# Five transposes per feature block of x, the keys' bank copied by ScalarE, and a later split of the cached values

## The chip, the cores and the metric

The kernel runs on one core of a Trainium2 chip, in one launch. The metric is device time in microseconds (us), as the median of repeated executions. Shown beside it is one execution taken with the hardware profiler, whose rows are quoted below.

## What is computed

The reference is one inference step of a streaming encoder with one layer. Its parts, cut to what matters here:

```python
h = rmsnorm(x, norm_attn_g)                       # x: 16 meta + 512 prompt rows, and 64 sample rows, 2048 features
z = h @ w_in                                      # columns: qd | kd | vd (8 heads x 128 each) | cq | ckv | krope
# group A: differential attention, 8 heads, two 64-wide halves each
s = einsum(qd, kd) * DIFF_SCALE + t5_bias         # chunk-causal mask; the sample also reads 128 cached keys
p = softmax(s)[half 0] - lam * softmax(s)[half 1]
o_d = rmsnorm(p @ vd) * (1 - lam_init)
# group B: latent attention with a rotary key; then
x = x + concat(o_d, o_m) @ w_out
x = x + (silu(h2 @ w_gate) * (h2 @ w_up)) @ w_down
y = rmsnorm(x)
# outputs: y, and the new rows of kd, vd, ckv and krope in their natural layout (tokens x columns)
```

All arithmetic is in fp32. The kernel forms each fp32 product from three faster ones of split operands (high times high, high times low, low times high).

## The kernel before

All 592 tokens (512 prompt, 64 sample, 16 meta) are kept as columns: a feature block is a tile of 128 features x 592 tokens. The change touches the first quarter of the program.

**The x stage** (`load_x`, `transpose_x`, `project_both`). Rows of x are loaded in groups of 512 features into tiles `xn`. For each of the 16 feature blocks, `transpose_x` lets TensorE transpose the pieces of x into one PSUM tile `pxt` of two banks, with half of the tokens (296) at the start of each bank. That is why there are six pieces: 128, 128, 40 tokens in the first bank, 108, 108 and 80 in the second. ScalarE then writes the scaled high part `xh`, VectorE the low part `xl` and a plain copy `xt`, which goes to memory (`xspill`). Two `pxt` tiles exist, so a block's transposes wait until VectorE has copied the `xt` of two blocks ago. ScalarE also squares the pieces (`junk`) for the row sums of the norm; `ss`, reduced by VectorE after the last group, becomes the factor `rc` per token. Between the transposes TensorE projects the first head's queries and keys (`ps`).

**The row factors** (`first_rows`). TensorE turns `rc` into rows (`prb`), one product for each piece, VectorE copies them to `rb`, and every projection is multiplied by it.

**A head of group A.** `projections` emits, for each head, the products of queries, keys and values in eight-block halves. Beside it run tasks: `twin_queries` and `stack_keys` split operands into high and low parts (`q00h`, `q00l`, `kk`); `keys` and `values` call `natural`, which transposes the new rows back to tokens x columns, copies the full bank of the 512 prompt tokens to `na` and stores it (`pna`, `na`), then does the same with the 80 other tokens (`pnb`, `nb`); `diff_attend` makes scores (`sp`, two banks), exponentials (`e`), probabilities (`p`) and products with the values (`po`). The transposes of `natural`, the cached keys' (`pck`), the probabilities' and the gains' (`pg`) share one PSUM bank, called "tp".

**What sets the order.** TensorE's order is the program's: a planner, `Streams`, keeps a model clock and picks the next task by rank and by the time its buffers are due, and TensorE's instructions are kept in that order. The other engines' instructions are placed by the compiler's scheduler, which uses its own costs. Each engine then works through its list in order, and waits at the head of it. Loads and stores go out on SP's queue, which is also in order; GpSimd issues the broadcasts of the bias table (`tsk<-trow`, one for each head), from which `bias` is loaded.

Of the kernel before, what the change touches and what calls it, by code (L numbers as in the profile page):

```python
# [116 lines left out]
def encoder_step(  # L117
# [181 lines left out]
    def ev(ps, n=TH):  # L299
        return ps[:, :, 0:n]  # L300
# [18 lines left out]
    with ExitStack() as ph:  # L319
# [33 lines left out]
        tok = [(0, P), (P, P), (256, 40), (TH, 108), (404, 108), (SEQ, OWN)]  # L353
        ps0, ps1 = pjt(), pjt()
        with tc.tile_pool(name="xn", bufs=1, reuse_waits="tile") as xn:
            first_gain = xn.tile([KC, P], F32, name="first_gain")
            S.dma_start(first_gain, g_attn.rearrange("(c p) -> c p", p=P))
            ssp = az.tile([P, 6, 4], F32, name="ssp")
# [4 lines left out]
            def load_x(cg):  # L363
                cs = slice(cg * 512, (cg + 1) * 512)
                for j in (0, 1, 2, 3, 5):
                    o, n = tok[j]
                    t = xn.tile([P, 1 + (j == 3), 512], F32, name="xn", tag=f"xn{j}", bufs=3)
                    second_queue = S.dma_start if cg == 0 and j in (1, 2, 5) else load
                    if j == 5:
                        second_queue(t[0:NS, 0], x_sample[:, cs])  # L370
                        second_queue(t[NS:OWN, 0], meta[:, cs])
                    elif j == 3:
                        load(t[0:n], x_prompt[o:o + 2 * n, cs].rearrange("(a p) c -> p a c", p=n))
                        xt_in[cg, 4] = t[:, 1]
                    else:
                        second_queue(t[0:n, 0], x_prompt[o:o + n, cs])
                    xt_in[cg, j] = t[:, 0]

            def transpose_x(kc):
                cg, k = kc // 4, kc % 4  # L380
                sp = sbig("pxt")
                for j, (o, n) in enumerate(tok):
                    b = o // TH
                    PE.transpose(sp[:, b, o - b * TH:o - b * TH + n],
                                 xt_in[cg, j][0:n, k * P:(k + 1) * P], ident[0:n, 0:n])
                xt = ztile("xt")
                split_scaled(hv(xh[kc]), hv(xl[kc]), ev(sp), gA[:, kc:kc + 1])
                V.tensor_copy(hv(xt), ev(sp))
                for o, n, c in KEPT:
                    store(xspill[kc, :, c:c + n], xt[:, o:o + n])  # L390
                for j in ((0, 1), (2, 3), (4,), (5,))[k]:
# [55 lines left out]
            ss = az.tile([P, 6], F32, name="ss")  # L447
            rc = az.tile([P, 6], F32, name="rc")
# [31 lines left out]
        def natural(src32, dst_p, dst_s, keep):  # L480
# [6 lines left out]
            V.tensor_copy(na, pa.rearrange("p (j c) -> p j c", j=4))  # L487
# [13 lines left out]
        def keys(h, z, kk):  # L501
# [4 lines left out]
            yield from natural(z, nk_p[:, c], nk_s[:, c], lambda na, nb: None)  # L506
# [22 lines left out]
        def values(h, z, vh, vl):  # L529
# [3 lines left out]
            split(vh[:, 5, :], vl[:, 5, :], cv)  # L533
# [1159 lines left out]
```

## Time and profile before

| | |
|---|---|
| median of 3 runs | 2409.49 us (2408.25 to 2411.52) |
| the profiled execution | 2406.11 us, its span 2404.3 us |
| busy in the span: TensorE, VectorE, ScalarE, GpSimd | 98%, 78%, 47%, 31% |
| x stage with the first head's projections | from 0 us to the first `prb` at 67.44 us |
| the eight heads of group A | from there to about 530 us |
| latent attention, output projection, feed-forward | from about 530 us to the end |

A row in order of time gives start, duration, engine, line, operation and tiles, and in brackets how long the engine stood idle before and what ended that. A row of a group gives count, busy time, mean in ns, and idle time ahead of it. Matmuls overlap, so the time that one holds TensorE's list is read from the start of the next, not from its duration.

### The profile page before, as it was taken

What the parts mean: (1) busy time and instruction counts of PE and PEld (TensorE: products, weight loads), DVE (VectorE), ACT (ScalarE), POOL (GpSimd) and SP (SyncE); (2) the same over time, 40 slices, a digit from 0 to 9 for tenths busy, and PEclk for the clock granted to TensorE, in tenths of its full rate; (3) what the DMA queues carried; (4) which work ended last, traced back from release to release, by engine and by line L of the source; (5) the groups of instructions that cost most, each with busy time, mean ns of one, the idle gap of its engine ahead of it and who ended that gap; (6) DMA issues with size and microseconds to landing.
All of it is one profiled execution on the core that took longest, in us unless ns stands there. A gap on an engine that the chain in (4) does not pass through costs nothing. (4 is left out here: it accounts for less than half of the span.)

```text
span 2404.3 us, 43647 instructions
## 1 busy us (share of the span) xinstructions
PE 2344.6 (98%) x17336; PEld 2305.3 (96%) x17336; DVE 1886.0 (78%) x2750; ACT 1127.8 (47%) x1999; POOL 740.7 (31%) x463
## 2 busy tenths in 40 slices
PE   7999999999999999999999999999999999999998
PEld 6999999989998999999999999999999999999997
DVE  5666677676665788888888888888888788888884
ACT  5455554444444554444445545445444333333435
POOL 0100000130000356465455455555554222222220
PEclk9999999999999999999999999999999999999999
DMA  7533333253333543444454454445345984744522
GB/s 217 146 91 96 85 89 96 75 155 118 112 103 108 179 150 116 155 158 130 151 165 135 140 165 147 138 155 162 127 151 174 323 285 145 242 164 152 193 89 97
DMA packets 360372, 353.10 MB, mean 147 GB/s; under 512 B 23906, under 2 KB 316392, under 8 KB 360168
## 3 DMA queue, kind: packets, MB, share of 16 engines
q1 hardware_dynamic: 358374, 345.47, 45.5%
q0 software_dynamic: 1296, 4.07, 0.5%
q8 instruction: 136, 2.23, 0.4%
q10 hardware_dynamic: 498, 0.78, 0.1%
q14 instruction: 68, 0.56, 0.1%
HBM read 268.82 MB, written 82.34 MB: 146 GB/s over the span
## 5 line engine op out<-in xcount | busy, mean ns | idle before, releaser
L1234 PE MATMUL m<-b,wh 128*128 128x288 f32 x7280 | 1061.6, 294 | 6.2 <-ACT wh L157 2.9
L1234 PEld LDWEIGHTS m<-b,wh 128*128 128x128 f32 x7280 | 995.4, 188 | 9.0 <-ACT wh L157 4.9
L1238 PE MATMUL m<-b,wl 128*128 128x288 f32 x3640 | 583.2, 296 | 4.3 <-DVE wl L154 3.0
L154 DVE TENSOR_TENSOR wl<-raw,wh 128x1024 fp32r<-128x1024 f32 (+2 forms) x347 | 509.5, 1469 | 40.7 <-ACT wh L157 40.3
L1238 PEld LDWEIGHTS m<-b,wl 128*128 128x128 f32 x3640 | 514.3, 188 | 10.2 <-DVE wl L154 9.1
L157 ACT ACTIVATE wh<-raw 128x1024 fp32r<-128x1024 f32 (+2 forms) x347 | 313.6, 904 | 367.2 <-PE m L1234 320.1
L1220 POOL TENSOR_TENSOR ws<-raw 128x512 f32<-128x512 f32 (+2 forms) x124 | 224.9, 1814 | 615.3 <-DVE wl L154 361.2
L157 ACT ACTIVATE wh<-ws 128x512 fp32r<-128x512 f32 (+2 forms) x248 | 196.6, 793 | 284.9 <-PE m L1234 113.6
L154 DVE TENSOR_TENSOR wl<-ws,wh 128x512 fp32r<-128x512 f32 (+2 forms) x248 | 250.1, 1008 | 7.7 <-PE m L1238 4.4
L109 PE MATMUL ps<-xh,wh 128*128 128x296 f32 (+1 forms) x992 | 223.8, 307 | 1.6 <-DVE ls L586 1.2
L109 PE MATMUL ps<-xl,wh 128*128 128x296 f32 (+1 forms) x992 | 215.8, 299 | 0.5 <-DVE xl L162 0.5
L109 PE MATMUL ps<-xh,wl 128*128 128x296 f32 (+1 forms) x960 | 208.0, 298 | 0.0
L1384 DVE TENSOR_TENSOR c<-c,s 128x288 fp32r<-128x288 f32 x172 | 170.8, 993 | 0.0
L1492 DVE TENSOR_TENSOR y<-y,m 128x288 f32<-128x288 f32 x280 | 125.7, 449 | 50.5 <-PE m L1238 50.5
L109 PEld LDWEIGHTS ps<-xh,wh 128*128 128x128 f32 x992 | 160.7, 190 | 4.3 <-ACT wh L157 1.4
L109 PEld LDWEIGHTS ps<-xl,wh 128*128 128x128 f32 x992 | 161.5, 189 | 0.9 <-DVE xl L162 0.9
L109 PEld LDWEIGHTS ps<-xh,wl 128*128 128x128 f32 x960 | 156.0, 189 | 0.0
L1220 POOL TENSOR_TENSOR raw<-raw 128x1024 f32<-128x1024 f32 (+1 forms) x46 | 143.2, 3114 | 3.5
L157 ACT ACTIVATE wh<-wr 128x1024 fp32r<-128x1024 f32 (+1 forms) x110 | 101.6, 924 | 87.2 <-PE ps L109 58.6
L154 DVE TENSOR_TENSOR wl<-wr,wh 128x1024 fp32r<-128x1024 f32 (+1 forms) x108 | 116.0, 1074 | 28.9 <-ACT wh L157 26.8
L1330 DVE TENSOR_TENSOR c<-c,m 128x288 f32<-128x288 f32 x171 | 73.1, 447 | 77.9 <-PE m L1238 47.7
L1403 POOL TENSOR_TENSOR c<-c,rb 128x576 f32<-128x576 f32 x44 | 74.9, 1703 | 138.1 <-ACT c L1402 138.1
(364 smaller groups left out, 3030.1 us busy)
## 6 DMA issues: line engine op xcount, KB each, us to landing
raw<-in_ffn_w_gate SPq DMA_DIRECT2D x44, 1024.0 KB, 9.3
raw<-in_ffn_w_up SPq DMA_DIRECT2D x44, 1024.0 KB, 7.3
b<-opspill SPq DMA_DIRECT2D x147, 288.0 KB, 6.0
raw<-in_ffn_w_down SPq DMA_DIRECT2D x32, 1024.0 KB, 5.7
wr<-in_w_in SPq DMA_DIRECT2D x57, 512.0 KB, 4.0
opspill<-s SPq DMA_DIRECT2D x43, 576.0 KB, 3.1
opspill<-c SPq DMA_DIRECT2D x43, 576.0 KB, 5.7
raw<-in_ffn_w_down SPq DMA_DIRECT2D x8, 1280.0 KB, 6.2
```

The source lines that it names most:

```text
L109: self.tc.keep_in_program_order(self.pe.matmul(out, lhsT, rhs, start=start, stop=stop))
L154: V.tensor_tensor(lo, src, f32(hi), op=ALU.subtract)
L157: S.activation(hi, src, AF.Copy)
L1220: (G if p in (5, 7) else V).tensor_tensor(x, y, z, op=ALU.add if p == 5 else ALU.subtract)
L1234: PE.matmul(banks[p], wh[:, k, :], x, start=first and new and k == 0 and x is hi, stop=False, skip_group_check=not new)
L1238: PE.matmul(banks[p], wl[:, k, :], hi, start=False, stop=last and k == n - 1, skip_group_check=not new)
L1330: V.tensor_tensor(c, c, banks[p], op=ALU.add)
L1384: V.tensor_tensor(src[:, k].bitcast(F32R), src[:, k], f32(hi[:, k]), op=ALU.subtract))
L1403: G.tensor_tensor(g[:, f, :], g[:, f, :], rb2, op=ALU.mult)
L1492: V.tensor_tensor(c, c, banks[p], op=ALU.add)
```

## The change

Three edits.

1. x is cut into five pieces of 128, 128, 128, 128 and 80 tokens, placed one after the other in `pxt` (512 columns in the first bank, 80 in the second). So a feature block has five transposes in place of six, a group of 512 features is loaded with two large and two small transfers (in the first group four of 128 rows, two of them from ScalarE's queue), there are 20 squares in place of 24, and `first_rows` makes five products in place of six and copies 512 and 80 columns in place of 296 and 296.
2. `natural` is handed its copy: for keys the full bank `pna` is copied to `na` by ScalarE, for values by VectorE as before.
3. In `values`, the split of the cached values `cv` is written at the end of the task, not after its load.

```diff
@@ -350,45 +350,42 @@
         V.memset(ones, 1.0)
 
 
-        tok = [(0, P), (P, P), (256, 40), (TH, 108), (404, 108), (SEQ, OWN)]
+        tok = [(0, P), (P, P), (2 * P, P), (3 * P, P), (SEQ, OWN)]
         ps0, ps1 = pjt(), pjt()
         with tc.tile_pool(name="xn", bufs=1, reuse_waits="tile") as xn:
             first_gain = xn.tile([KC, P], F32, name="first_gain")
             S.dma_start(first_gain, g_attn.rearrange("(c p) -> c p", p=P))
-            ssp = az.tile([P, 6, 4], F32, name="ssp")
+            ssp = az.tile([P, 5, 4], F32, name="ssp")
             V.memset(ssp, 1.0)
             junk = xn.tile([P, 512], F32, name="junk")
             xt_in = {}
 
             def load_x(cg):
                 cs = slice(cg * 512, (cg + 1) * 512)
-                for j in (0, 1, 2, 3, 5):
-                    o, n = tok[j]
-                    t = xn.tile([P, 1 + (j == 3), 512], F32, name="xn", tag=f"xn{j}", bufs=3)
-                    second_queue = S.dma_start if cg == 0 and j in (1, 2, 5) else load
-                    if j == 5:
-                        second_queue(t[0:NS, 0], x_sample[:, cs])
-                        second_queue(t[NS:OWN, 0], meta[:, cs])
-                    elif j == 3:
-                        load(t[0:n], x_prompt[o:o + 2 * n, cs].rearrange("(a p) c -> p a c", p=n))
-                        xt_in[cg, 4] = t[:, 1]
+                for j in (0, 2):
+                    t = xn.tile([P, 2, 512], F32, name="xn", tag=f"xn{j}", bufs=3)
+                    if cg:
+                        load(t, x_prompt[j * P:(j + 2) * P, cs].rearrange("(a p) c -> p a c", p=P))
                     else:
-                        second_queue(t[0:n, 0], x_prompt[o:o + n, cs])
-                    xt_in[cg, j] = t[:, 0]
+                        for i, queue in enumerate((load, S.dma_start)):
+                            queue(t[:, i], x_prompt[(j + i) * P:(j + i + 1) * P, cs])
+                    xt_in[cg, j], xt_in[cg, j + 1] = t[:, 0], t[:, 1]
+                t = xt_in[cg, 4] = xn.tile([OWN, 512], F32, name="xn", tag="xn4", bufs=3)
+                second_queue = load if cg else S.dma_start
+                second_queue(t[0:NS], x_sample[:, cs])
+                second_queue(t[NS:OWN], meta[:, cs])
 
             def transpose_x(kc):
                 cg, k = kc // 4, kc % 4
-                sp = sbig("pxt")
+                sp = sbig("pxt").rearrange("p a b -> p (a b)")[:, 0:T]
                 for j, (o, n) in enumerate(tok):
-                    b = o // TH
-                    PE.transpose(sp[:, b, o - b * TH:o - b * TH + n],
-                                 xt_in[cg, j][0:n, k * P:(k + 1) * P], ident[0:n, 0:n])
+                    PE.transpose(sp[:, o:o + n], xt_in[cg, j][0:n, k * P:(k + 1) * P], ident[0:n, 0:n])
                 xt = ztile("xt")
-                split_scaled(hv(xh[kc]), hv(xl[kc]), ev(sp), gA[:, kc:kc + 1])
-                V.tensor_copy(hv(xt), ev(sp))
+                split_scaled(xh[kc], xl[kc], sp, gA[:, kc:kc + 1])
+                V.tensor_copy(xt, sp)
                 for o, n, c in KEPT:
                     store(xspill[kc, :, c:c + n], xt[:, o:o + n])
-                for j in ((0, 1), (2, 3), (4,), (5,))[k]:
+                for j in ((0,), (1,), (2,), (3, 4))[k]:
                     n = tok[j][1]
                     S.activation(junk[0:n], xt_in[cg, j][0:n], AF.Square, accum_out=ssp[0:n, j, cg:cg + 1])
                 if kc == 3:
@@ -444,8 +441,8 @@
                 project_both(kc)
                 if kc + 2 < KC:
                     transpose_x(kc + 2)
-            ss = az.tile([P, 6], F32, name="ss")
-            rc = az.tile([P, 6], F32, name="rc")
+            ss = az.tile([P, 5], F32, name="ss")
+            rc = az.tile([P, 5], F32, name="rc")
             V.reduce_sum(ss, ssp, axis=AX.X)
             V.tensor_scalar(ss, ss, 1.0 / D, EPS, op0=ALU.mult, op1=ALU.add)
             rsqrt(rc, ss)
@@ -477,14 +474,14 @@
         p5 = ap.tile([P, 2 * P], F32, name="p5")
         G.memset(p5, 0.0)
 
-        def natural(src32, dst_p, dst_s, keep):
+        def natural(src32, dst_p, dst_s, keep, copy):
 
             yield from st.take("tp")
             pa = tbank("pna")
             for j in range(4):
                 PE.transpose(pa[:, j * P:(j + 1) * P], src32[:, j * P:(j + 1) * P], ident)
             na = ap.tile([P, 4, P], F32, name="na", tag="na")
-            V.tensor_copy(na, pa.rearrange("p (j c) -> p j c", j=4))
+            copy(na, pa.rearrange("p (j c) -> p j c", j=4))
             store(dst_p[NM:NM + SEQ, :].rearrange("(j p) c -> p j c", p=P), na)
             st.give("tp", 1.9)
             yield 1.0
@@ -503,7 +500,8 @@
             ck = ap.tile([P, P], F32, name="ck", tag="ck", bufs=2)
             load(ck, cache_k[:, c])
             yield 2.0
-            yield from natural(z, nk_p[:, c], nk_s[:, c], lambda na, nb: None)
+            yield from natural(z, nk_p[:, c], nk_s[:, c], lambda na, nb: None,
+                               lambda out, bank: S.activation(out, bank, AF.Copy))
             yield from st.take("tp")
             pk = tbank("pck")
             PE.transpose(pk[:, 0:P], ck, ident)
@@ -530,7 +528,6 @@
             c = slice(h * P, (h + 1) * P)
             cv = ap.tile([P, P], F32, name="cv", tag="ck", bufs=2)
             load(cv, cache_v[:, c])
-            split(vh[:, 5, :], vl[:, 5, :], cv)
             yield 1.2
 
             def keep(na, nb):
@@ -538,7 +535,8 @@
                 stack_own(vh[:, 0, :], nb[0:NS])
                 meta_values(vmt[h % 2], nb[NS:OWN])
 
-            yield from natural(z, nv_p[:, c], nv_s[:, c], keep)
+            yield from natural(z, nv_p[:, c], nv_s[:, c], keep, V.tensor_copy)
+            split(vh[:, 5, :], vl[:, 5, :], cv)
             yield 1.5
 
         rows = 23
@@ -690,11 +688,11 @@
                 yield from st.take("po")
                 banks = [tbank("prb"), pso.tile([P, 512], F32, name="prb", tag="po")]
                 for j, (o, n) in enumerate(tok):
-                    b = o // TH
-                    PE.matmul(banks[b][:, o - b * TH:o - b * TH + n], rc[0:n, j:j + 1].to_broadcast([n, P]),
+                    b = j // 4
+                    PE.matmul(banks[b][:, o - b * SEQ:o - b * SEQ + n], rc[0:n, j:j + 1].to_broadcast([n, P]),
                               ident[0:n, 0:n], start=True, stop=True)
-                for b, name in enumerate(("tp", "po")):
-                    V.tensor_copy(rb[:, b * TH:(b + 1) * TH], banks[b][:, 0:TH])
+                for b, (name, cols) in enumerate((("tp", slice(0, SEQ)), ("po", slice(SEQ, T)))):
+                    V.tensor_copy(rb[:, cols], banks[b][:, 0:cols.stop - cols.start])
                     st.give(name, 2.0)
                 queries(0, ps0)
                 yield 3.0
```

How the lists of the engines change, at three places.

ScalarE, key task of head 3 (`kk` are the stacked keys, `e` the exponentials of head 2, `wh` weights). Before:

```order
L518 ACTIVATE kk_2363<-z 64x16
L518 ACTIVATE kk_2364<-z 64x16
L581 ACTIVATE e,ls<-e,nm 128x272 x2
L495 ACTIVATE nb<-pnb 80x128
L581 ACTIVATE e,ls<-e,nm 128x400
L157 ACTIVATE wh<-wr 128x1024
L581 ACTIVATE e,ls<-e,nm 128x400
L518 ACTIVATE kk_2363<-pck 64x128
L518 ACTIVATE kk_2364<-pck 64x128
```

Now:

```order
L516 ACTIVATE kk_2328<-z 64x16
L516 ACTIVATE kk_2329<-z 64x16
L579 ACTIVATE e,ls<-e,nm 128x272
L504 ACTIVATE na<-pna 128x512
L579 ACTIVATE e,ls<-e,nm 128x272
L492 ACTIVATE nb<-pnb 80x128
L579 ACTIVATE e,ls<-e,nm 128x400
L157 ACTIVATE wh<-wr 128x1024
L579 ACTIVATE e,ls<-e,nm 128x400
L516 ACTIVATE kk_2328<-pck 64x128
```

The copy of the bank stands between the two exponentials of 272 columns; it has left VectorE's list. The same holds in heads 4 to 7.

VectorE, first head (`trs` is the bias table's two halves, `pg` the bank that waits for them, `kk` keys and `q00l`, `q01l` queries). Before:

```order
L526 TENSOR_TENSOR q00l<-z,q00h 64x576
L675 COPY trs_713<-ptr 8x328
L675 COPY trs_714<-ptr 8x328
L519 TENSOR_TENSOR kk_805<-z,kk_805 64x576
L519 TENSOR_TENSOR kk_806<-z,kk_806 64x576
L519 TENSOR_TENSOR kk_805<-z,kk_805 64x16
L519 TENSOR_TENSOR kk_806<-z,kk_806 64x16
L526 TENSOR_TENSOR q00l<-z,q00h 64x576
L683 COPY gT<-pg 128x23
L526 TENSOR_TENSOR q01l<-z,q01h 64x576
L684 TENSOR_SCALAR gT<-gT 128x1
```

Now:

```order
L524 TENSOR_TENSOR q00l<-z,q00h 64x576 x2
L517 TENSOR_TENSOR kk_768<-z,kk_768 64x576
L517 TENSOR_TENSOR kk_769<-z,kk_769 64x576
L517 TENSOR_TENSOR kk_768<-z,kk_768 64x16
L517 TENSOR_TENSOR kk_769<-z,kk_769 64x16
L673 COPY trs_679<-ptr 8x328
L673 COPY trs_680<-ptr 8x328
L524 TENSOR_TENSOR q01l<-z,q01h 64x576
L681 COPY gT<-pg 128x23
L524 TENSOR_TENSOR q01l<-z,q01h 64x576
L682 TENSOR_SCALAR gT<-gT 128x1
```

Both copies `trs` moved behind the second `q00l` and all four `kk`.

GpSimd, the broadcasts of the bias table and the first wait behind them (`bias`). Before:

```order
L676 DMA trow<-trs_713 8x328
L676 DMA trow<-trs_714 8x328
L549 DMA tsk<-trow 128x656 x6
L556 MEMSET bias 64x64
L549 DMA tsk<-trow 128x656 x2
L556 MEMSET bias 64x64
```

Now:

```order
L674 DMA trow<-trs_679 8x328
L674 DMA trow<-trs_680 8x328
L547 DMA tsk<-trow 128x656 x7
L554 MEMSET bias 64x64
L547 DMA tsk<-trow 128x656
L554 MEMSET bias 64x64
```

Seven broadcasts in place of six are issued ahead of the first `bias` instruction, which waits for a load.

## The prediction

> **What bounds the kernel now.** I read the page first, then the busy time by stretches, then who TensorE waits for, and then the rows in order of time at each place that the change touches.
>
> ```profile
> span 2404.3 us, 43647 instructions
> PE 2344.6 (98%) x17336; PEld 2305.3 (96%) x17336; DVE 1886.0 (78%) x2750; ACT 1127.8 (47%) x1999; POOL 740.7 (31%) x463
> 0.00:60.00 60.00, 44.32 (x271) 38.36 (x272) 30.47 (x49) 34.39 (x73) 5.09 (x15) 0.94 0.77 217
> 300.00:600.00 300.00, 290.40 (x2148) 285.17 (x2148) 211.70 (x453) 140.05 (x293) 33.66 (x27) 1.00 0.38 107
> PE pnb L113 <- DVE na L487: 7.4, 5, 1.5
> ```
>
> In the second row TensorE (PE) is busy 98% of the span, in the fourth 290 of 300 us: what sets the end is TensorE's own list, in program order, plus its gaps. Two sorts of edit can pay: fewer products on that list, or a gap closed. The stretch rows give busy time of PE, weight loads, DVE, ACT and POOL, then granted clock, DMA share and GB/s: the first 60 us hold 15.7 of the 60 us that TensorE idles. The last row is a gap with a name: five times 1.5 us the transpose into `pnb` waits for VectorE's copy `na`, which the change gives to ScalarE for keys.
>
> **The key copies (heads 3 to 7).** One head in order of time (start, duration, engine; in brackets the idle time before):
>
> ```profile
> 211.13 0.60 PE L113 MATMUL pna<-ident,z 128*128 128x128 f32 x4
> 211.48 0.52 PE L109 MATMUL ps<-xh,wh 128*128 128x296 f32 x2
> 214.11 0.43 PE L109 MATMUL ps<-xh,wl 128*128 128x296 f32 x2
> 216.04 0.31 PE L113 MATMUL pnb<-ident,z 128*80 128x128 f32 x1 [1.49 <-DVE na L487]
> 214.21 0.43 DVE L577 CUSTOM_DVE_ANT_0 e<-sp,bias 128x272 f32<-128x272 f32 x1
> 214.57 0.81 DVE L620 SCALAR_TENSOR_TENSOR o<-o,gT,r 128x576 f32<-128x576 f32 x1
> 215.30 0.68 DVE L487 COPY na<-pna 128x512 f32<-128x512 f32 x1
> 211.26 0.52 ACT L581 ACTIVATE e<-e,nm 128x272 f32<-128x272 f32 x1
> 214.68 0.52 ACT L581 ACTIVATE e<-e,nm 128x272 f32<-128x272 f32 x1 [2.81 <-DVE nm L577]
> ```
>
> The bank `pna` is full at 211.73, VectorE copies it only at 215.30, behind work that has nothing to do with it, and TensorE stands from 214.55 to 216.04. ScalarE is idle for 2.81 us between its two 272-wide exponentials, and the new order puts the copy exactly there. No row shows ScalarE doing this 128x512 copy; the row for its 128x512 squares below says 626 ns, VectorE's own 680. So it ends near 212.5, 2 us before TensorE asks: the 1.49 us go. Behind the copy in ScalarE's list stands the second exponential, which waits for VectorE until 214.65 anyway, so nobody waits for the waiting copy. On SP's queue the store of `na` now comes ahead of the store of `o` into `mspill`; neither has a reader near: 0. What is late next: the score product behind `pnb` needs the bank that VectorE's 272-wide read frees at 214.64, where TensorE would now stand at 214.41, so 0.25 us can come back. Per head 1.24 to 1.49; five heads 6.2 to 7.4; I take **6.7**. The hiding work is ScalarE's idle time; without it eight copies of 0.65 would cost 5.2. VectorE is relieved of the same eight, which is no gain by itself.
>
> **Five transposes per block.** Rows of the x stage:
>
> ```profile
> 21.76 0.97 PE L113 MATMUL pxt<-ident,xn 128*128 128x128 f32 x6
> 22.52 0.51 PE L109 MATMUL ps<-xh,wh 128*128 128x288 f32 x2
> 40.80 1.60 PE L113 MATMUL pxt<-ident,xn 128*128 128x128 f32 x6 [2.80 <-DVE ss L168]
> 38.08 0.63 ACT L393 ACTIVATE junk<-xn 108x512 f32<-108x512 f32 x1
> 38.84 0.63 ACT L393 ACTIVATE junk<-xn 80x512 f32<-80x512 f32 x1
> 39.59 0.18 DVE L449 TENSOR_REDUCE ss<-ssp 128x6 f32<-128x24 f32 x1 [1.28 <-ACT junk L393]
> 39.88 0.77 DVE L388 COPY xt<-pxt 128x592 f32<-128x592 f32 x1
> L393 ACT ACTIVATE junk<-xn 128x512 f32<-128x512 f32 (+3 forms) x24 | 15.0, 626 | 0.4
> 20.00:30.00 10.00, 9.29 (x69) 8.41 (x67) 5.10 (x7) 8.87 (x22) 0.00 (x0) 1.00 0.90 251
> 30.00:40.00 10.00, 7.59 (x54) 6.73 (x54) 5.65 (x10) 9.24 (x23) 0.15 (x1) 1.00 0.80 234
> 40.00:50.00 10.00, 9.20 (x47) 8.18 (x48) 5.91 (x10) 3.31 (x6) 0.39 (x1) 0.66 0.58 173
> ```
>
> Six transposes hold the list for 22.52 - 21.76 = 0.76 us. Four of full width took 211.48 - 211.13 = 0.35 us above. The fifth, 80 wide, is bounded by 0.03 (what is left over) and 0.2 (a quarter of the six is 0.19); I take 0.16, five in 0.51, so 0.25 per block and 4.0 over 16. But not all of it counts. TensorE's restart at 40.80 is not set by TensorE: VectorE's reduction of the sums of squares (39.59) waits for ScalarE's last square, and the copies that free the PSUM tile stand behind it; the changed order still has the reduction ahead of them. ScalarE is the full engine there, 8.87 and 9.24 of 10 us. It has 24 squares and will have 20; from the starts 38.08 and 38.84 one costs 0.76, so the restart comes 4 x 0.76 = **3.0** earlier, and the transposes saved before it only make TensorE wait as long as now. From the restart on seven blocks count, 7 x 0.25 = **1.75**. The row sums `prb` (12 products in 1.77, first row below) become 10: **0.3**. Together 5.05. Bounds: 3.3 if five cost what six do, 7.9 if the 2.80 us stall went too, for which nothing in the rows speaks.
>
> [...]
>
> The loads of x (4 for a group of 512 features where there were 6, other than in the first) only fill SP's queue less. At the start ScalarE's queue carries 176 KB more ahead of the sample's rows and SP's 176 KB less; at 217 GB/s that is 0.8 us either way, taken as nothing since the squares set the restart.
>
> **What the new order costs in heads 0 and 1.**
>
> ```profile
> 67.44 1.77 PE L109 MATMUL prb<-ident,rc 128*128 128x128 f32 x12
> 73.57 0.89 DVE L675 COPY trs<-ptr 8x328 f32<-8x328 f32 x2
> 74.48 1.89 DVE L519 TENSOR_TENSOR kk<-z,kk 64x576 fp32r<-64x576 f32 x4
> 76.39 0.75 DVE L526 TENSOR_TENSOR q00l<-z,q00h 64x576 fp32r<-64x576 f32 x1
> 75.39 0.27 PE L113 MATMUL pg<-ident,gains 128*128 128x128 f32 x1
> 77.96 3.19 POOL L549 DMA_DIRECT2D tsk<-trow  x6 [2.62 <-DMA trow<-trs]
> 93.70 0.31 ACT L157 ACTIVATE vh<-cv 128x128 fp32r<-128x128 f32 x1 [6.87 <-DMA cv<-in_cache_diff_v]
> 99.65 0.31 DVE L577 CUSTOM_DVE_ANT_0 e<-sp,bias 128x144 f32<-128x144 f32 x1
> 100.84 0.29 PE L109 MATMUL sp<-kk,q00h 128*128 128x272 f32 x1
> tsk<-trow POOLq DMA_DIRECT2D x8, 328.0 KB, 6.5
> 80.00:90.00 10.00, 8.78 (x68) 8.53 (x66) 2.41 (x5) 2.14 (x5) 1.15 (x3) 1.00 0.90 280
> ```
>
> Two things get worse. First, VectorE's copies `trs` move behind a second `q00l` and four `kk`: 0.75 + 1.89 = 2.6 later. `pg` needs their bank, and all of TensorE's list stands behind `pg`; before it had it 0.9 us early (74.46 against 75.39). So 2.6 - 0.9 = 1.7 of wait at most, nothing if VectorE keeps ahead; I take **+1.2**. Second, a chain that does not run on TensorE: `trs`, then `trow`, then the broadcasts `tsk` (one more, seven, now stands ahead of GpSimd's wait), which fill the DMA engines (0.90 busy at 280 GB/s), so that the cached values `cv` land at 93.70, and ScalarE, VectorE's first score read at 99.65 and TensorE's third score product at 100.84 follow. VectorE ends that read at 99.96, so TensorE has 0.88 us of slack there. The chain itself starts 5.05 - 2.6 = 2.4 earlier, less 328 KB / 280 GB/s = 1.2 for the broadcast. TensorE can therefore be ahead by 0.88 + 1.2 = 2.1 to 0.88 + 2.4 = 3.3 when head 0's scores are through; I take **2.7**, whatever it had won before (5.05 - 1.2 = 3.85). The split of `cv`, the third edit, stands in ScalarE's list as early as before relative to the transposes, with the copy of the new values now ahead of it; what waits behind it still waits: 0. If it freed the 6.87 us, the cap above would go, worth 1.1.
>
> **The sum.** 2.7 + 6.7 = 9.4 us. The profiled execution took 2406.11, so it would take 2396.7. The median of the runs shown is 2409.49, 3.4 above it, which I carry over: **2400.1**. What comes later is untouched and TensorE's, so nothing takes the gain back.
>
> **Rivals.**
>
> The clock. After the 2.80 us stall the granted clock is 0.66 over 40 to 50 us. The stretch at half speed that this means is 3.4 us lost in ten (10 x (1 - 0.66)). A new stall of two us in head 0 or 1, where 1.49 us did not trigger it, would add 3.4 or, twice, 6.8: 2403.5 to 2407. For: the cap leaves TensorE to stand 1.1 us or more in one piece. Against: the 300:600 row, with three of the 1.49 us gaps in it, has the clock at 1.00. 15%. The other way, the stall before 40.80 split in two and the clock kept: 2396.7, 10%. [...]
>
> The copy comes no earlier. If ScalarE's list runs late, so that the first exponential comes only where the second is now, the copy ends at 215.9, as VectorE's does, and the five gaps stay: 2409.5 - 2.7 = 2406.8. For: a strict list behind VectorE's results. Against: 2.81 us of idle. 10%.
>
> Slower: the same place, one step worse. If the copy stands behind both exponentials and the 400-wide one that follows, `pnb` moves to about 218.1, 2.1 later than now, in five heads +10.5, less 2.7: 2417. It decides from a copy that ends after 215.98. Against: the new order has it between the 272-wide two. 5%.
>
> **How the numbers follow.** Forecast 60% (2397 to 2403.5), rivals 15, 10, 10 and 5. What a measurement here can tell is about 0.2%, 4.8 us. Faster by more, under 2404.7: the forecast, the kept clock and half of the clock rival, 78%; within, 17%; slower, 5%. The range: lowest, 5.05 kept whole, 7.4 for the five heads and the clock kept, 15.8, 2393.7; highest, the gaps stay, 2406.8. So 2394 to 2407.
>
> **What would show it.** `pnb` no longer waits for `na` in heads 3 to 7, and `na<-pna` on ScalarE ends before 213 of the old clock. Five `pxt` take about 0.5 us. The stall ahead of the tenth block stays near 2.8 us and starts 3 us sooner. New waits: `pg` for VectorE, a score product of head 0 for VectorE. From head 7 on the two traces run 9 us apart to the end. It is wrong if the copy waits in ScalarE's list, or if the new waits in heads 0 and 1 pass 5 us together.

## The result, and the profile after

The changed kernel takes 2397.02 us as the median of its runs, against 2408.87 us for the kernel before on the same chip: ratio 0.9949, 95% interval 0.9929 to 0.9968. The forecast was 2400.1, the range 2394 to 2407. One of its four executions took 7189.5 us, three times as long as the others, and is left out of the ratio (without it the median would be 2396.5). A second measurement gave 2397.37 against 2408.34, ratio 0.9953 (0.9939 to 0.9967). The profiled execution's span went from 2404.3 to 2395.4 us, 8.9 less; the profiled execution of the kernel before, at 2406.11 us, lay 2.8 below its median.

First, from the views of the changed kernel: the page's head, then whom TensorE waits for (sum, times, longest).

```profile
span 2395.4 us, 43586 instructions
PE 2342.1 (98%) x17318; PEld 2305.0 (96%) x17318; DVE 1885.2 (79%) x2742; ACT 1128.0 (47%) x1999; POOL 742.6 (31%) x463
```

```profile
PE sp L109 <- DVE nm L575: 5.1, 3, 3.0
PE pxt L113 <- DVE ss L168: 2.5, 1, 2.5
PE pg L113 <- DVE trs L673: 0.3, 1, 0.3
```

The wait of `pnb` for `na`, five times 1.5 us before, is gone from the list. The stall ahead of the tenth block of x is still there (2.5 for 2.8). A new wait leads the list: score products that wait for VectorE, two of them 3.03 and 1.86 us long.

The stretches show where they lie (columns as in the prediction's rows):

```profile
20.00:30.00 10.00, 10.00 (x81) 9.92 (x79) 7.24 (x10) 9.84 (x25) 0.00 (x0) 1.00 0.72 198
...
90.00:100.00 10.00, 6.97 (x51) 6.68 (x50) 8.75 (x21) 6.69 (x14) 0.00 (x0) 1.00 0.36 92
...
300.00:600.00 300.00, 294.51 (x2166) 288.28 (x2165) 210.55 (x445) 140.95 (x295) 35.43 (x28) 0.99 0.38 108
```

TensorE is busy 10.0 of the ten us from 20 to 30 (9.29 before), and 294.5 of the 300 us from 300 to 600 (290.4 before); from 90 to 100 it idles 3 us that it did not idle before (9.48). How far the changed kernel is ahead, from the start of the same piece of TensorE's work in both traces:

| Place | before | changed | ahead |
|---|---|---|---|
| transposes of the tenth block (the restart) | 40.80 | 36.46 | 4.3 |
| row sums `prb` | 67.44 | 59.97 | 7.5 |
| gains `pg` | 75.39 | 68.72 | 6.7 |
| third score product of head 0 | 100.84 | 95.41 | 5.4 |
| keys' `pna` of head 3 | 211.13 | 206.27 | 4.9 |
| values' `pna` of head 7 | 426.38 | 415.50 | 10.9 |
| the end | 2404.3 | 2395.4 | 8.9 |

So the x stage won 7.5, heads 0 to 2 took 2.6 back, heads 3 to 7 won 6.0, and the rest of the program took 2.0. (The row of `pg` is lower than the one above it mainly because three pairs of products, 0.8 us, stand ahead of `pg` in the new order and stood behind it in the old one.) The prediction's two terms were 2.7 at head 3 and 6.7 from the five heads.

Head 3 in order of time, answering the rows that the prediction shows of it:

```profile
206.27 0.60 PE L113 MATMUL pna<-ident,z 128*128 128x128 f32 x4
209.53 0.27 PE L113 MATMUL pnb<-ident,z 128*80 128x128 f32 x1
209.85 0.46 PE L109 MATMUL sp<-kk,q01h 128*128 128x400 f32 x1
209.35 0.43 DVE L575 CUSTOM_DVE_ANT_0 e<-sp,bias 128x272 f32<-128x272 f32 x1
206.93 0.58 ACT L504 ACTIVATE na<-pna 128x512 f32<-128x512 f32 x1
209.83 0.52 ACT L579 ACTIVATE e<-e,nm 128x272 f32<-128x272 f32 x1 [2.32 <-DVE nm L575]
```

ScalarE copies the bank as soon as it is full and ends at 207.51, 2.0 us before TensorE asks with `pnb`. The score product behind `pnb` starts 0.26 later than the transpose lets it (0.32 behind it, 0.06 in the kernel before), since VectorE ends its 272-wide read at 209.78.

The x stage and the row sums:

```profile
19.25 0.75 ACT L161 ACTIVATE xh<-pxt,gA 128x592 fp32r<-128x592 f32 x1 [1.73 <-PE pxt L113]
20.70 0.67 PE L113 MATMUL pxt<-ident,xn 128*128 128x128 f32 x5
21.17 0.51 PE L109 MATMUL ps<-xh,wh 128*128 128x288 f32 x2
34.50 0.63 ACT L390 ACTIVATE junk<-xn 80x512 f32<-80x512 f32 x1
35.25 0.18 DVE L446 TENSOR_REDUCE ss<-ssp 128x5 f32<-128x20 f32 x1 [1.28 <-ACT junk L390]
36.46 1.22 PE L113 MATMUL pxt<-ident,xn 128*128 128x128 f32 x5 [2.50 <-DVE ss L168]
59.97 1.24 PE L109 MATMUL prb<-ident,rc 128*128 128x128 f32 x10
```

Five transposes hold the list for 21.17 - 20.70 = 0.47 us, where six held it for 0.76. The last square and the reduction come 4.3 us earlier, and the restart with them.

The chain through the bias table, and the two score products that end it:

```profile
68.18 0.89 DVE L673 COPY trs<-ptr 8x328 f32<-8x328 f32 x2
71.63 3.70 POOL L547 DMA_DIRECT2D tsk<-trow  x7 [1.67 <-issue]
80.97 0.53 SPq L138 DMA_DIRECT2D cv<-in_cache_diff_v  x1
88.83 0.31 ACT L157 ACTIVATE vh<-cv 128x128 fp32r<-128x128 f32 x1 [6.80 <-DMA cv<-in_cache_diff_v]
95.04 0.31 DVE L575 CUSTOM_DVE_ANT_0 e<-sp,bias 128x144 f32<-128x144 f32 x1
95.41 0.39 PE L109 MATMUL sp<-kk,q00h 128*128 128x272 f32 x1 [3.03 <-DVE nm L575]
110.18 0.39 PE L109 MATMUL sp<-kk,q01h 128*128 128x264 f32 x1 [1.86 <-DVE nm L575]
```

Link by link against the rows of before: `trs` 5.4 earlier, the first broadcast 6.3 earlier, `cv` of head 1 (it is the cached values of head 1 that ScalarE's list meets here) 4.9 earlier, VectorE's first score read 4.6 earlier, and the third score product 5.4 earlier. TensorE, 8.6 us ahead by then (its `pnb` of the new values starts at 81.93, 90.52 before), stands there until the chain arrives.

### The profile page after: what moved, and what is told of

It is laid out like the page before. It is cut to its first block, busy times and chain, and to the rows that moved or that the text cites. A ratio compares the mean times of both kernels' runs of the same rounds, so it can differ in the third digit from the quotient of the medians.

```text
span 2395.4 us, 43586 instructions
## 1 busy us (share of the span) xinstructions
PE 2342.1 (98%) x17318; PEld 2305.0 (96%) x17318; DVE 1885.2 (79%) x2742; ACT 1128.0 (47%) x1999; POOL 742.6 (31%) x463
```

## The experiments

All times are medians, each ratio against runs of the kernel before on the same chip. In the expectations "the ninth block" of the stall is the block whose transposes start at 36.46; counted from one it is the tenth, as in the prediction.

**The keys' copy alone taken back.**

```diff
             yield from natural(z, nk_p[:, c], nk_s[:, c], lambda na, nb: None,
-                               lambda out, bank: S.activation(out, bank, AF.Copy))
+                               V.tensor_copy)
```

> The changed kernel with the keys' full bank copied by VectorE again. Theory: the five gaps of heads 3 to 7 are VectorE's order alone, so the wait of pnb for na is back five times at about 1.5 us; the changed kernel's lead over the kernel before, 4.9 us at head 3, stays 4.9 to the end, so about 6.0 us are lost: 2397.0 + 6.0 = 2403.0, up to 1.2 more because eight broadcasts in place of seven now stand ahead of GpSimd's first wait. Rival: with the x stage moved, VectorE reaches the copy in time and the edit was worth little: under 2399.

Measured: 2402.55 against 2407.23, ratio 0.9981 (0.9972 to 0.9990). Who waits from 200 to 440 us, and the chain of head 0:

```profile
PE pnb L113 <- DVE na L484: 7.4, 5, 1.5
```

```profile
72.31 4.21 POOL L547 DMA_DIRECT2D tsk<-trow  x8 [1.65 <-issue]
...
91.03 0.31 ACT L157 ACTIVATE vh<-cv 128x128 fp32r<-128x128 f32 x1 [4.68 <-DMA cv<-in_cache_diff_v]
```

The five gaps are back to the tenth of a us: they belong to VectorE's list, whatever the x stage does. The rival falls. Eight broadcasts are ahead here, and `cv` is split 18.7 us behind the first of them (17.2 with seven). That the time is the forecast 2403 is in part luck: this trace is only 2.3 us ahead of the kernel before at head 3 (211.13 and 208.84), not 4.9, since in head 0 the values' `pnb` waits 2.94 us and half-speed stretches come at 86 and 113 us; heads 3 to 7 then win nothing, and the span is 2401.1 us, 5.7 more than the changed kernel's.

**The five pieces alone taken back** (the kernel before with the second and third edit).

```diff
-        tok = [(0, P), (P, P), (2 * P, P), (3 * P, P), (SEQ, OWN)]
+        tok = [(0, P), (P, P), (256, 40), (TH, 108), (404, 108), (SEQ, OWN)]
...
-                for j in ((0,), (1,), (2,), (3, 4))[k]:
+                for j in ((0, 1), (2, 3), (4,), (5,))[k]:
```

> The kernel before with the keys' copy on ScalarE and the late split of cv, but six transposes per block. Theory: x stage as before (restart at 40.8, prb at 67.4), no lead over 1 us at head 3, then 6.0 us from the five heads: 2408.9 - 6.0 = 2402.9, at best 0.9 less. Rival: what the x stage wins is lost anyway, because the third score product of head 0 waits for a transfer that does not come earlier; then this kernel is as fast as the changed one, 2397 to 2398.

Measured: 2399.82 against 2407.23, ratio 0.9971 (0.9961 to 0.9981): 7.4 us faster, not 6.0. Without the five pieces the x stage is as before (restart at 41.34), yet the trace is 3.8 us ahead at head 3 (0.8 of it already at the row sums, after a half-speed stretch of 3.41 us in place of 6.83).

```profile
76.98 3.18 POOL L550 DMA_DIRECT2D tsk<-trow  x6 [2.39 <-DMA trow<-trs]
86.02 0.69 DVE L487 COPY na<-pna 128x512 f32<-128x512 f32 x1 [1.94 <-DMA out<-na]
91.42 0.31 ACT L157 ACTIVATE vh<-cv 128x128 fp32r<-128x128 f32 x1 [4.05 <-DMA cv<-in_cache_diff_v]
```

Two waits of the kernel before in heads 0 and 1 are gone here. One is 1.75 us of the values' `pnb` in head 0. The tile `na` exists once: VectorE's copy of the new values waits until the keys' `na` is stored, at 89.78 before, at 86.02 here. The other is 0.91 us of head 1's `pck`; close behind it a transpose of probabilities now waits 0.56 us for `kk`, which it did not before. How much of this is the edit, and how much the order in which transfers landed, a further execution of each tells:

> The kernel before once more, for a second look at head 0. Theory: the 1.75 us for which the values' transposes wait for the store of the keys' bank belongs to the list (VectorE copies the keys' bank at 79.0 us, the store is issued behind six broadcasts), so it is there again, 1.3 to 2.2. Rival: it is a matter of the order in which transfers happen to land: under 1 or over 2.6 this time, with the third score product of head 0 standing for what is missing.

> Six transposes, the keys' copy on ScalarE and the late split once more. Theory: the lead over the kernel before at head 3 (3.8 us in the first look) comes from the copy being 1.2 us earlier in head 0, so that the store goes ahead of the broadcasts' bulk, and from the wait of 0.9 us for nb in head 1 that goes: 3.4 to 4.2 again, no wait in head 0. Rival: the cached values happened to land early (14.4 us behind the first broadcast, against 15.7 in the kernel before); then they land after 15.2 this time, and the lead is under 3.

In the further execution of the kernel before, the wait for the store is 1.06 us in place of 1.75. In that of this kernel the cached values are split at 92.54, 14.9 us behind the first broadcast in place of 14.4 (14.7 and 15.7 in the kernel before), the values' `pnb` of head 0 waits 0.36 us for the store, and at head 3's `pna` this execution leads that of the kernel before by 1.6 us (210.06 and 208.42), not 3.8. So the theory falls; of the rival the smaller lead came, the late landing did not. More than half of the 3.8 us of one pair of traces is chance. The wait of 0.9 us for `nb` in head 1 does go with the edit both times, and the new one for `kk` (0.54) comes both times. Its time, 2399.70 in that one execution, is the same as in the first measurement, so 7.4 us stand, of which heads 3 to 7 account for 6; where the rest comes from is not settled beyond the 0.4 that these two waits leave.

**Fewer broadcasts ahead of the bias loads.** Only GpSimd's list changes.

```diff
-            if h + 2 < H:
-                skew(h + 2)
             bias = ap.tile([P, 528], F32, name="bias")
             load(bias, skewed(h, 127, P, 528))
-            G.memset(bias[0:64, 464:528], -BIG)
+            tc.keep_in_program_order(G.memset(bias[0:64, 464:528], -BIG))
+            if h + 2 < H:
+                skew(h + 2)
```

(and the broadcast in `skew` is kept in program order in the same way).

> The changed kernel with only two broadcasts of the bias table ahead of GpSimd's first bias instruction in place of seven, and one more behind each later one; every other engine's list is the same. Theory: cv of head 1 lands late (88.8 us, 7.8 us after its load was issued) because seven broadcasts of 328 KB fill the DMA engines; with two it lands before 83, the waits of 3.03 us (third score product of head 0) and 1.86 us (head 1) go below 0.5 together, and the half-speed stretch at 111 us goes with them: 4.9 to 6.6 us off 2397.0, 2390.4 to 2392.1. Rival: cv is late because its load stands behind the three bias loads in SP's queue and shares the engines with a weight load of 512 KB; then it lands after 87 and the time is 2396 to 2397.

Measured: 2390.01 against 2407.23, ratio 0.9932 (0.9920 to 0.9945).

```profile
72.30 1.12 POOL L547 DMA_DIRECT2D tsk<-trow  x2 [1.63 <-issue]
...
82.64 0.29 ACT L157 ACTIVATE vh<-cv 128x128 fp32r<-128x128 f32 x1
90.42 0.31 DVE L575 CUSTOM_DVE_ANT_0 e<-sp,bias 128x144 f32<-128x144 f32 x1
```

The load of 512 KB of weights that stands ahead of `bias` and `cv` in SP's queue, with its time from issue to landing, in the changed kernel and here:

```profile
wr<-in_w_in SPq DMA_DIRECT2D x1, 512.0 KB, 13.7
...
wr<-in_w_in SPq DMA_DIRECT2D x1, 512.0 KB, 6.7
```

Nobody waits for `cv` any more, VectorE's first score read comes 4.6 us earlier, the stall of 3.03 us is gone and that of 1.86 is 0.78; so is the half-speed stretch at 111 us. The rival falls as a forecast. A part of it is right all the same: in both traces `cv` lands behind those weights and behind the three loads of `bias`, in the order of SP's queue (87.39, then 88.22 to 88.62, then 88.81 us in the changed kernel; 81.11, 81.92 to 82.25 and 82.42 here). What the broadcasts hold up is the whole queue, the weights first. The five broadcasts that went out early cost the changed kernel 5 to 6 us (17.2 us faster than before here, 11.9 and 11.0 there).

**The same with six transposes.** The six-piece kernel above with the edit of the broadcasts.

> Six transposes per block, the keys' copy on ScalarE, the late split, and two broadcasts ahead in place of six. Beside the five-piece kernel with two broadcasts (2390.0, before 2407.2) it tells what the x stage is worth when nothing in head 0 takes it back. Theory: with six pieces TensorE's lead is too small for the transfer to stop it (no score product waits in head 0 of the six-piece kernel with six broadcasts, 2399.8), so two broadcasts win little here: 2398 to 2400, and the x stage is worth 8 to 10 us of the time with its own lead of 6.5, against 2.9 with seven broadcasts. Rival: the broadcasts cost TensorE some 5 us whatever its lead: 2393 to 2395, and the x stage is worth 3 to 5 with two broadcasts as with seven.

Measured: 2399.10 against 2408.07, ratio 0.9962 (0.9950 to 0.9975), no better than with six broadcasts. The forecast came, but the transfer did not come earlier: `cv` is split at 91.43 us here (91.42 and 92.54 with six broadcasts), behind a weight load issued at 85.24 that took 6.0 us. In neither of the two six-piece kernels does the third score product of head 0 wait. So a transfer as late as this costs nothing while TensorE is late too; what an earlier one would be worth with six pieces, this run does not show. The trace with five pieces and two broadcasts is 7.0 us ahead of this one at the row sums and still 6.7 at 445 us (the same projection starts at 445.99 and 452.70), where the changed kernel, with seven broadcasts, had 4.9 us of its 7.5 left at head 3. In time the x stage is worth 8.2 us here (17.2 against 9.0 faster than before), as the theory had it.

**The split of `cv` early again.**

```diff
             load(cv, cache_v[:, c])
+            split(vh[:, 5, :], vl[:, 5, :], cv)
...
             yield from natural(z, nv_p[:, c], nv_s[:, c], keep, V.tensor_copy)
-            split(vh[:, 5, :], vl[:, 5, :], cv)
```

> The changed kernel with the split of cv written after its load again. Theory: in head 1 ScalarE's list only swaps the copy of the new values with the split of cv, and everything behind both waits for the same transfer, so the time is that of the changed kernel within 2 us: 2395 to 2399, ratio to the kernel before 0.994 to 0.996. Rival: the swap lets the values' bank and its high part go ahead of a transfer that lands 6.8 us late, and the edit carries a part of the gain: 3 us or more slower than the changed kernel, ratio above 0.9962.

Measured: 2396.09 against 2408.07, ratio 0.9951 (0.9937 to 0.9964). The third edit is worth nothing that can be measured. In this execution the values' `pnb` waited 1.68 us for the store of `na` and the third score product 1.45, together 3.13. The changed kernel once more, to see how the two share:

> The changed kernel once more. Theory: the waits of head 0 (store of the keys' bank, third score product) together come from the seven broadcasts and are 3.0 to 3.2 us in sum, however they are shared between the two places (0 and 3.03 in the first look, 1.68 and 1.45 with the split of cv early); the time 2395 to 2398, ratio 0.994 to 0.996. Rival: the sum differs by over 0.8 us from one execution to the next.

It was 1.06 and 2.07 there, again 3.13; in the profile above 0 and 3.03. The theory holds for these three: the chain sets one end, and which wait pays is chance. In the two traces with seven broadcasts and a changed x stage below, the sum is 2.4 (1.93 and 0.46, 2.11 and 0.27).

**The stall of the x stage.** Is it VectorE's order? The reduction is put behind the last copy `xt`:

```diff
-                V.tensor_copy(xt, sp)
+                tc.keep_in_program_order(V.tensor_copy(xt, sp))
...
-            V.reduce_sum(ss, ssp, axis=AX.X)
+            tc.keep_in_program_order(V.reduce_sum(ss, ssp, axis=AX.X))
```

> The changed kernel with VectorE's reduction of the sums of squares behind its last copy xt, in place of ahead of the copies of the eighth and ninth block. Theory: the stall ahead of the ninth block is those copies standing behind the reduction, which waits for ScalarE's last square; moved, the stall falls from 2.50 to about 0.7 and the half-speed stretch that follows it (3.4 us, 1.7 lost) does not come: prb 3.5 us earlier. The chain to cv of head 1 starts at the row sums and moves along, so the wait in head 0 does not take it back: 2393.5. Rival: the stall has its cause in the order of ScalarE's squares and stays: 2397. Second rival: it goes, and the third score product of head 0 stands longer by the same: 2397 too, with prb 3.5 earlier.

Measured: 2394.79 against 2407.23, ratio 0.9952 (0.9940 to 0.9965): no different from the changed kernel.

```profile
34.10 0.83 DVE L162 SCALAR_TENSOR_TENSOR xl<-pxt,gA,xh 128x592 fp32r<-128x592 f32 x1 [0.94 <-ACT xh L161]
35.76 1.48 DVE L385 COPY xt<-pxt 128x592 f32<-128x592 f32 x2 [0.82 <-DMA xspill<-xt]
36.68 0.52 PE L113 MATMUL pxt<-ident,xn 128*128 128x128 f32 x3 [1.76 <-DVE xt L385]
```

The stall shrinks to 1.76, not to 0.7: with the reduction out of the way the copy waits for the store of an older `xt`. No half-speed stretch follows it, and the trace is 1.2 us ahead of the changed kernel at the row sums (58.78 and 59.97), not 3.5. The values' `pnb` then waits 1.93 us for the store, and later in this execution TensorE ran at half speed for 24 us in all (20.5 in the changed kernel). Neither the theory's 2393.5 nor its sizes came.

Is it the number of squares? Sixteen in place of twenty:

```diff
-                for j in ((0,), (1,), (2,), (3, 4))[k]:
+                for j in ((0,), (1,), (2,), (4,))[k]:
```

> The changed kernel with 16 squares in place of 20 (it leaves out the squares of the fourth piece, so those tokens' row factors are not those of the norm). Theory of the prediction: ScalarE's squares set the restart ahead of the ninth block, 0.76 us each, so four fewer bring the reduction 3.0 us earlier, at 32.2 of the span in place of 35.25, and the stall of 2.50 us goes below 0.5; the half-speed stretch does not come. Rival: TensorE's own transposes and VectorE's copies set the restart, which then stays within 1 us of 36.5.

```profile
28.82 0.76 ACT L161 ACTIVATE xh<-pxt,gA 128x592 fp32r<-128x592 f32 x1 [1.42 <-PE pxt L113]
35.49 0.18 DVE L446 TENSOR_REDUCE ss<-ssp 128x5 f32<-128x20 f32 x1 [0.73 <-ACT junk L390]
36.70 0.52 PE L113 MATMUL pxt<-ident,xn 128*128 128x128 f32 x3 [1.95 <-DVE ss L168]
```

The restart does not move (36.70; 36.05 to 37.14 in the five traces with twenty and the same place of the reduction; 2397.11 in one execution). ScalarE now waits for TensorE's transposes instead, 1.42 us in one piece. So with twenty squares the two are about even: the theory holds from 24 to 20 and not below, and the rival holds here.

Last, both causes at once: two broadcasts, the reduction late, and each block's squares kept behind its own `xh`, so that they do not stand ahead of the tenth block.

```diff
-                    S.activation(junk[0:n], xt_in[cg, j][0:n], AF.Square, accum_out=ssp[0:n, j, cg:cg + 1])
+                    tc.keep_in_program_order(
+                        S.activation(junk[0:n], xt_in[cg, j][0:n], AF.Square, accum_out=ssp[0:n, j, cg:cg + 1]))
```

(the activation that writes `xh` is kept in program order too).

> Two broadcasts ahead, and ScalarE's squares kept behind the high part of their own block, so that they are spread over all sixteen blocks in place of standing ahead of the tenth, with the reduction behind VectorE's last copy xt. Theory: ScalarE is full between 20 and 35 us only because all 20 squares stand ahead there; spread, the stall of 2.50 us falls below 0.5 and no half-speed stretch follows (1.7), the row factors come after the sixteenth block in time for prb or up to 1 us late: 2390.0 - 2.5 - 1.7 + 0..1 = 2385.8 to 2386.8. Rival: the stores of xt set the restart (with the reduction late VectorE's copy waited 0.82 us for one), the stall stays at 1 to 1.8, or prb waits 2 us or more for its factors: 2388 to 2390.

Measured: 2386.75 against 2408.07, ratio 0.9910 (0.9895 to 0.9925), the fastest of all and faster than both kernels of this case.

```profile
35.22 0.70 PE L113 MATMUL pxt<-ident,xn 128*128 128x128 f32 x5 [1.10 <-DVE xt L386]
57.04 1.24 PE L109 MATMUL prb<-ident,rc 128*128 128x128 f32 x10
```

The stall is 1.10 us, no half-speed stretch comes in the first 500 us, and the row sums start 10.4 us earlier than before, with their factors in time. The time came as forecast; the stall did not: it stayed in the range of the rival (1 to 1.8), and VectorE's copy `xt` waits here too for the store of an older one, 0.22 us. So that the time fits is in part luck, and how much of the 3.3 us over the kernel with two broadcasts alone (2390.0) belongs to the squares and how much to the reduction, no run separates.

## Why the prediction was right

The time was forecast 3.1 us too long and held by the range. The mechanism was right for the key copies and for the cap in head 0, and one step of the x stage was wrong; the errors of the sizes partly cancelled. In the pair of traces the lead at head 3 was 2.2 us larger than taken, the five heads won 0.7 less and the rest of the program took 2.0 that was taken as nothing: 8.9 in place of 9.4. That the sum came so near is luck in part.

- **The key copies.** Right. The five gaps went, and they come back when the copy does. The copy took 0.58 us (estimate 0.626) and ended 2.0 us before TensorE asked. The 0.25 us that could come back did, 0.26 in head 3; the rest of the head cost another 0.2, so five heads won 6.0 (10.9 - 4.9) where 6.7 was taken, just under the range of 6.2 to 7.4. "Neither has a reader near" held for heads 3 to 7. In head 0 the store of `na` has one, VectorE's next copy into the one tile; the step left that out.
- **Five transposes.** A block won 0.76 - 0.47 = 0.29 against 0.25. Much of that is probably not the number of pieces but their unequal rows: pieces of 128 rows start 0.11 us apart in both kernels, while in the kernel before the step from 128 rows to 40 took 0.20 us and the one from 40 to 108 took 0.18. What a row of six equal pieces would take, no run shows.
- **The restart.** "The transposes saved before it only make TensorE wait as long as now" is the step that failed here. The restart came 4.3 us earlier, not 3.0. In the kernel before ScalarE had itself stood for TensorE's transposes while it was called full:

```profile
20.30 0.76 ACT L161 ACTIVATE xh<-pxt,gA 128x592 fp32r<-128x592 f32 x1 [1.35 <-PE pxt L113]
22.77 0.75 ACT L161 ACTIVATE xh<-pxt,gA 128x592 fp32r<-128x592 f32 x1 [0.34 <-PE pxt L113]
25.21 0.76 ACT L161 ACTIVATE xh<-pxt,gA 128x592 fp32r<-128x592 f32 x1 [0.32 <-PE pxt L113]
```

  After the change it starts the first of these at 19.25, the third at 24.04, and does not stand again until the last square. From the third to the reduction it took 14.4 us before and 11.2 now: 3.2 for the four squares. The other 1.2 us came earlier, from TensorE's side, and 0.8 of them before any projection ran. The first projection, before and after:

```profile
14.88 0.85 PE L109 MATMUL ps<-xh,wh 128*128 128x288 f32 x2 [0.38 <-ACT xh L161]
...
14.05 0.85 PE L109 MATMUL ps<-xh,wh 128*128 128x288 f32 x2 [1.52 <-ACT xh L161]
```

  It starts 0.83 earlier here, between 13.80 and 14.38 in all eight traces with five pieces and between 14.88 and 15.25 in the five with six. What comes before it is the loads of x and of the first weights and two blocks of transposes: the prediction took its 0.8 us of loads "as nothing since the squares set the restart". No run separates the loads from the pieces. The sixteen squares show the same from the other side. The x stage won 7.5 up to the row sums and 8.0 with them, where 5.05 was taken; 1.7 of that is a half-speed stretch that was shorter in this execution (below).
- **The wait of `pg`.** It came, 0.33 us, where 1.2 was taken. `trs` ended 3.8 us behind the start of `ptr` against 2.0 before (69.07 - 65.28, 74.46 - 72.46), 1.8 more and not 2.6.
- **The cap in head 0.** Right in every link, and the place where the largest size was wrong. The chain was taken to start at most 2.4 us earlier; the first broadcast went out 6.3 us earlier (71.63 against 77.96). The reasons are the x stage (7.2 us at the start of `ptr`, 2.1 more than taken), the 0.8 of `trs`, and 1.0 us less between `trow` and its reader (1.67 for 2.62). The broadcast that was added cost 6.3 - 4.9 = 1.5 in this pair, taken as 1.2; over all traces `cv` is split 14.4 to 15.7 us behind the first of six and 16.8 to 18.3 behind the first of seven, 2.4 apart in the mean. So head 3 was reached 4.9 ahead, taken as 2.7. That the broadcasts are the cause is shown: two in place of seven take the stall away and 5 us of time or more. They act through SP's queue, where `cv` stands behind weights that they slow.
- **The third edit.** Nothing, as predicted.
- **The clock.** The rival (15%) happened in its kind and not in its price: after the waits in heads 0 and 1 a half-speed stretch came at 111 us. It lasted 3.41 us and cost 1.7, not 3.4. Half-speed time between the start and the end of the program is 20.5 us in both traces: before, 6.83 in the x stage and 13.65 at 774 and 785 us; in the changed kernel 3.41 each in the x stage, at 111 and at 524 us, and 10.24 at 767 and 777. The stretch at 524 is most of the 2.0 us that "what comes later is untouched" missed: around it the lead falls from 10.9 to 9.3.
- **The other rivals** fell: the copy came early on ScalarE, and no exponential stood ahead of it.

## What to carry to other kernels

A gain ahead of a wait is worth only what the other chain into that wait moves; follow that chain link by link, price what is put into its transfer queues, and ask what it will be when the first engine is faster. An engine that is 90% busy may still be waiting for the one it is said to hold up (ScalarE, busy 8.87 of the ten us from 20 to 30 before the change, stood 0.34 and 0.32 us there for TensorE's transposes), so two limits that are nearly even both have to be moved. And issue large transfers that are needed late only when they are needed: five broadcasts sent early held up a queue with two transfers that TensorE was to wait for, the store of `na` and the load of `cv` (the weights ahead of `cv` took 13.7 us to land, 6.7 without the five).

## What was not expected of the hardware

**Half-speed stretches of 3.41 us or twice that.** In the traces of both kernels every stretch at a granted clock of 0.50, but for the last, in which the program ends, lasts 3.41 or 6.83 us, and within one execution their starts lie whole multiples of 3.41 us apart (36.15, 111.24, 524.25, 766.60 and 776.84 us in the changed kernel; 40.45, 774.31 and 784.55 before). Four pieces of the changed kernel, cut in that step:

```profile
90.76:94.17 3.41, 1.62 (x12) 1.37 (x11) 3.04 (x4) 3.35 (x5) 0.00 (x0) 1.00 0.33 94
94.17:97.58 3.41, 2.17 (x15) 2.13 (x16) 2.64 (x10) 1.61 (x6) 0.00 (x0) 1.00 0.54 146
107.83:111.24 3.41, 1.55 (x13) 1.31 (x12) 3.03 (x10) 1.64 (x4) 0.00 (x0) 1.00 0.71 189
111.24:114.65 3.41, 3.41 (x16) 3.35 (x16) 1.59 (x4) 0.83 (x2) 0.14 (x1) 0.50 0.46 121
```

The longer stall, 3.03 us, is cut by this step into 1.79 and 1.24 us of idle time (3.41 less the busy time), and the clock stays at 1.00. The shorter one, 1.86 us, falls into one piece, which is left with 1.55 busy, and the next runs at 0.50. From 20 to 500 us, in pieces cut like this, those at full speed that were followed by one at 0.50 had 2.43 us of idle time in the kernel before and 2.18 and 1.86 in the changed kernel; the most idle of those that were not had 1.75 and 1.79. In the further execution of the changed kernel a piece with 2.07 was followed by one at 0.50, and one with 1.90 by two:

```profile
32.04:35.45 3.41, 1.51 (x12) 1.27 (x10) 1.41 (x4) 2.90 (x8) 0.35 (x1) 1.00 0.61 190
35.45:38.86 3.41, 2.81 (x13) 2.84 (x14) 2.31 (x7) 0.98 (x3) 0.20 (x1) 0.50 0.93 291
38.86:42.27 3.41, 3.41 (x16) 3.39 (x16) 0.94 (x3) 0.98 (x2) 0.00 (x0) 0.50 0.41 118
```

The first of the two has 0.60 us of idle time. Before, a piece at 0.50 with 0.35 was followed by another at 0.50; in the changed kernel one with 0.31 was followed by full speed. At 0.50 the transposes of 128 rows start 0.21 us apart (36.70 to 37.34 us in the changed kernel), for 0.11 at 1.00. So in the two executions of the changed kernel the stall ahead of the tenth block was followed by 3.41 and by 6.83 us at half speed, an estimated 1.7 and 3.4 us lost, and the stall of the third score product by none where it lasted 3.03 us and by 3.41 or more where it lasted 2.07. Beyond 500 us, where TensorE's work is of other kinds, a piece with 1.39 us of idle time was followed by one at 0.50 in the kernel before, and one with 1.73 was not; what else counts there stays open. That the idle time within such a piece decides is the author's reading of these traces; no run was made to test it.

**A queue slowed by another queue's transfers.** In the changed kernel's list the 64 KB of `cv` were split 16.8 to 18.3 us behind the first of seven broadcasts (five executions with that list in head 0), and 10.3 us behind the first of two, where nobody waited: at least (17.2 - 10.3) / 5 = 1.4 us for each broadcast of 328 KB, though the broadcasts go out on another queue than `cv`. An estimate from 280 GB/s had given 1.2. It is not a price of `cv` alone: the 512 KB of weights ahead of it took 13.3 to 14.8 us to land with seven broadcasts, 6.2 and 6.7 with two and 4.0 as the median of the program, and `cv` landed 1.3 to 1.4 us behind them in the changed kernel and with two broadcasts. With six pieces, where the weights were issued later, two broadcasts in place of six brought `cv` no more than 1 to 1.5 us nearer to the first of them (13.4 behind it, 14.4 and 14.9 with six).
